# The opening of a two-block transformer layer: the adaptive scale computed on TensorE, products before the norm is known, no GpSimd

## The chip, the cores and the metric

One core of a Trainium2 chip. The metric is the device time of one execution in microseconds (us). All data is fp32; 268 MB of weights are read once from device memory.

## The reference

`reference` runs two blocks on x (256 tokens by 1024 features). Only the start of the first block is touched:

```
ada = silu(c) @ w_ada + b_ada                 # 1024 -> 6 x 1024
sh1, sc1, g1, sh2, sc2, g2 = split(ada, 6)
h = rms_norm(x, norm1_pre) * (1 + sc1) + sh1
proj = h @ w_in                               # ... q, k (512 each), v (1024), c/b/x gates, o, i, f, ga, gm
qk = silu(causal_dwconv(concat(q, k), conv_qk_w))     # 4 taps
```

rms_norm divides each token by the root of its mean square, so it is one factor r per token. The mLSTM over q, k, v, the rest of the mixer, the PEER layer with 16384 experts and the whole second block follow, and the change leaves them as they are.

## The kernel before

Features lie on the 128 partitions, in 8 groups j (or k) of 128; a tile 128x256 is one group of all 256 tokens. Every weight matrix comes from device memory in pieces of 128x1024 fp32 (512 KB). ScalarE rounds a piece to its high part `wh`, VectorE or GpSimd subtracts to get the low part `wl` (`split`, L160), and TensorE makes three products per 128x128 square: `wh`·`hh`, `wh`·`hl`, `wl`·`hh` (`mm3`, L182), where `hh` and `hl` are the two parts of h. 24 such matmuls of 256 columns are one output of 128 features (`gemm`, L189).

The opening is a list of steps, `ORD` (L25), run at L556 in that order; the planner of the language then orders each engine's queue by its own estimate of when an instruction can start.

- `load_c` (C, L461): silu(c) as one row on one partition, ten small matmuls on ones (`F0`), and four matmuls of one row that spread it over all partitions into `crow`.
- `load_x` (X, L500): x, its squares and their sum over features, the factor r per token (L318), and `u` = x·r for the 8 groups on VectorE (L506).
- `load_shift` (B0 to B7, L536) and `load_scale` (S0 to S7, L524): each loads a 128x1024 piece of `w_ada` (rows are features, so the product with silu(c) is a sum along the row) and VectorE multiplies it by `crow` and adds up (`product`, L423). B gives 128 shifts, S gives 128 scales. S then sets gain A1 (L526), ScalarE makes `u`·A1 + B1 (L528) and the high part (L532), GpSimd the low part (L532).
- `load_w` (W0 to W5, L508): pieces of the q and k weights; GpSimd makes five of the six low parts (`WG`, L30). `FL` (L27) adds filler matmuls behind some loads.
- `some` (H, L544): the outputs 0 to 3 group by group as the groups of h come, then 4 and 5.

`ORD2` (L26, run at L650) is what follows: w0, w1 load and split pieces 6 and 7 of the q and k weights; q6, q7 are their outputs; u0 to u7 are the units that take an output out of the accumulator, convolve it over four taps and apply silu (`unit_qk`, L577, with `conv`, L571); v0 to v3 compute v from 8 pieces (`wide`, L195), of which GpSimd makes the low part of every second one (`PV`, L29); l0 and g0 are the gates. Outputs 0, 1, 6, 7 and all of v share two accumulator banks with the name `mm`. After that comes the loop at L717 over the pieces `wcxb`, and from there on the kernel is a long row of such products.

Of the kernel before, what the change touches and what calls it, by code (L numbers as in the profile page):

```python
# [8 lines left out]
F32 = mybir.dt.float32  # L9
F32R = mybir.dt.float32r  # L10
# [102 lines left out]
def body(ctx: ExitStack, tc: tile.TileContext, a: dict):  # L113
# [298 lines left out]
    with ExitStack() as p1:  # L412
# [4 lines left out]
        A.dma_start(out=col, in_=a["cols"])  # L417
        A.dma_start(out=cst["a"], in_=a["ca"])

        def big(name, slot, dt=F32):  # L420
            return f8.tile([128, 8, 256], dt, tag=f"s{slot}", name=name)

        def product(raw, j):  # L423
            scr = m1.tile([128, 1024], F32, tag="adas", name="scr", bufs=2)
# [3 lines left out]
        def adapt():  # L428
            for b in range(16):
                raw = m1.tile([128, 2048], F32, tag="araw", name="araw", bufs=2)  # L430
                SY.dma_start(out=raw, in_=a["wada"][8 + b])
# [12 lines left out]
        u = big("u", 5)  # L444
        qz = big("qz", 2)
        G.memset(qz, 0.0)
# [6 lines left out]
        def bct():  # L453
            return bank("bc", 256)

        banks = [bank(t) for t in ("sc", "num", "den", "ssq", "bc")]
        psb = bank("psb")

        early = []

        def load_c():  # L461

            c1, t1 = (m1.tile([128, 1024], F32, tag="adas", name=n, bufs=2)[:1] for n in ("c1", "t1"))
            tc.keep_in_program_order(SY.dma_start(out=c1, in_=a["c"]))
            A.activation(t1, c1, AF.Tanh, scale=0.5)
            V.scalar_tensor_tensor(out=c1, in0=t1, scalar=1.0, in1=c1, op0=ALU.add, op1=ALU.mult)
            for n in range(F0):
                T.matmul(psb[:, :128], lhsT=ones, rhs=ones, start=True, stop=True)
            for i in range(2):
                early[:] = [T.matmul(banks[i], lhsT=ones[:1, :], rhs=c1[:, i * 512:(i + 1) * 512], start=True, stop=True)]  # L470
                A.copy(crow[:, i * 512:(i + 1) * 512], banks[i])
# [6 lines left out]
        def warm(key, raw):  # L478

            for n in range(FL.get(key, 0)):  # L480
                T.matmul(psb[:, :256], lhsT=ones, rhs=raw[:, n * 256:(n + 1) * 256], start=True, stop=True)

        where = dict(B0=4, B2=8, B4=0, B6=0, S0=6, S2=7, S4=3, S6=0)
        stage = {}

        def adaload(src, t, n):
            b = f"{t}{n & 6}"
            if n % 2 == 0:
                if where[b]:
                    stage[b] = f8.tile([128, 2048], F32, tag=f"s{where[b]}", name="araw")  # L490
                else:
                    stage[b] = m1.tile([128, 2048], F32, tag="araw", name="araw", bufs=2)
            raw = halfload(stage[b], src[n // 2], n % 2)
            warm(f"{t}{n}", raw)
            return raw

        raws = [sp.tile([128, 2048], F32, tag="raw", name="raw", bufs=3) for _ in range(3)]
        ws, more = [], []

        def load_x():  # L500
            tc.keep_in_program_order(SY.dma_start(out=x, in_=a["xT"].rearrange("p (j t) -> p j t", j=8)))
            with tc.issue_after(early[0].ins):
                sums(m1, banks[4], x, presum(m1, x))
                r1 = norm(m1, banks[4])[0]
            for j in range(8):
                V.tensor_mul(u[:, j, :], x[:, j, :], r1)  # L506

        def load_w(n):  # L508
            p = halfload(raws[n // 2], a["wqk"][n // 2], n % 2)
            warm(f"W{n}", p)  # L510
            if n < 4:
                ws.append(split(p, G if WG >> n & 1 else V))
                return
            t = f8.tile([128, 2048], F32R, tag=f"s{(4, 8)[n - 4]}", name="w4")
            with tc.issue_after(made[0].ins), tc.issue_after(made[1].ins):
                A.copy(t[:, :1024], p)
                (G if WG >> n & 1 else V).tensor_sub(t[:, 1024:], p, t[:, :1024].bitcast(F32))
            more.append((t[:, :1024], t[:, 1024:]))

        A1, B1, one = (m1.tile([128, 8], F32, name=n) for n in ("A1", "B1", "one"))  # L520
        V.tensor_scalar_add(one, col[:, bo + 8:bo + 16], 1.0)
        V.tensor_mul(one, one, KS("n1pre"))

        def load_scale(n):  # L524
            product(adaload(a["wada"][4:], "S", n), 8 + n)
            V.scalar_tensor_tensor(out=A1[:, n:n + 1], in0=ada[:, 8 + n:9 + n], scalar=K("n1pre", n), in1=one[:, n:n + 1],  # L526
                                   op0=ALU.mult, op1=ALU.add)
            A.activation(u[:, n, :], u[:, n, :], AF.Identity, scale=A1[:, n:n + 1], bias=B1[:, n:n + 1])  # L528
            parts_of_h(n)

        def parts_of_h(j):
            made[:] = [A.copy(hh[:, j, :256], u[:, j, :]), G.tensor_sub(hl[:, j, :256], u[:, j, :], hh[:, j, :256].bitcast(F32))]  # L532

        made = []

        def load_shift(n):  # L536
            product(adaload(a["wada"], "B", n), n)

        def shift():
            V.tensor_add(B1, ada[:, 0:8], col[:, bo:bo + 8])  # L540

        pss = [mmt(), mmt()] + [b[:, :256] for b in banks[:4]]

        def some():  # L544

            for k in range(8):
                n = slice(k * 128, (k + 1) * 128)
                for i, (x_, w_) in enumerate(((hh, 0), (hh, 1), (hl, 0))):
                    for ps, w in zip(pss, ws):
                        T.matmul(ps, lhsT=w[w_][:, n], rhs=x_[:, k, :256], start=k == 0 and i == 0,  # L550
                                 stop=k == 7 and i == 2)
            for ps, w in zip(pss[4:], more):
                gemm(ps, w, hh, hl)

        raw3 = sp.tile([128, 2048], F32, tag="raw", name="raw", bufs=3)
        for t in ORD.split():  # L556
            {"X": load_x, "C": load_c, "W": load_w, "S": load_scale, "B": load_shift, "F": shift,
             "H": some}[t[0]](*[int(v) for v in t[1:]])
        bg = []
        bg_ada = [adapt()]  # L560

# [87 lines left out]
        cst["b"] = m1.tile([128, NCST["b"]], F32, name="cb")  # L649
        for t in ORD2.split():  # L650
            n = int(t[1])
            if t[0] == "w":
                w67 = split(halfload(raw3, a["wqk"][3], n))
            elif t[0] == "l":
                wif = m1.tile([128, 8, 72], F32, name="wif")
                tc.keep_in_program_order(SY.dma_start(out=wif, in_=a["wif"].rearrange("p (k n) -> p k n", k=8)))
                SY.dma_start(out=cst["b"], in_=a["cb"])
            elif t[0] == "q":
                pss.append(mmt())
                gemm(pss[-1], w67, hh, hl)  # L660
            elif t[0] == "u":
                unit_qk(pss[n], n)
            elif t[0] == "v":
# [769 lines left out]
def layout(x, c, w_ada, b_ada, norm1_pre, norm1_post, w_in, conv_a_w, conv_qk_w, b_igate, b_fgate, mh_norm_w,  # L1433
# [27 lines left out]
    r["wada"] = ca(w.reshape(1024, 24, 2, 128).transpose(1, 3, 2, 0)).reshape(24, 128, 2048)  # L1461
    r["c"] = n(c)
    cols = np.zeros((128, NCOL), np.float32)

    def put(name, v):
# [72 lines left out]
```

## Time and profile before

| | us |
|---|---|
| three runs: median (lowest to highest) | 1509.54 (1508.81 to 1511.1) |
| the profiled execution, its time | 1508.95 |
| span of its instructions | 1507.2 |
| TensorE busy over the span | 1453.8 |
| VectorE busy | 1156.4 |
| ScalarE busy | 906.3 |
| GpSimd busy | 107.2 |

The profile is of one execution. An engine's busy time says how much of the span it worked; the rows further down say when, what ended its waits, and at which clock TensorE ran. PE is TensorE's matmuls, PEld its weight loads, DVE VectorE, ACT ScalarE, POOL GpSimd.

### The profile page before, as it was taken

The numbers are of one execution on the slowest core, as the hardware profiler recorded it, in microseconds if no ns is written. First come the engines' busy times: TensorE is split into PE (matmuls) and PEld (weight loads), VectorE is DVE, ScalarE is ACT, GpSimd is POOL, SyncE is SP. The second block draws the span as 40 slices with busy tenths as digits, with TensorE's granted clock in tenths as the row PEclk, the third lists the DMA queues.
The fourth block names the chain that finished last, engine by engine and source line by source line (L and its number), as shares of the span: only waits on it lengthen the run. The fifth ranks groups of instructions, "written<-read, shape, count | busy, mean of one in ns | idle before, by whom it ended". The sixth has DMA issues, their size and how long they took to land.

```text
span 1507.2 us, 27126 instructions
## 1 busy us (share of the span) xinstructions
PE 1453.8 (96%) x11020; PEld 1324.7 (88%) x11020; DVE 1156.4 (77%) x2154; ACT 906.3 (60%) x1242; POOL 107.2 (7%) x55
## 2 busy tenths in 40 slices
PE   5899999998998799999999999999999999999998
PEld 4889899997998799999878998777788899899897
DVE  8978797667998927787999887888865679575554
ACT  3554354445543547888877777787755569554543
POOL 3310000004231430000000000000000000000000
PEclk8999999999999999999999999999999999999999
DMA  9556667553434364544455545554555643345542
GB/s 349 182 201 231 229 251 255 181 180 119 169 140 168 112 200 166 169 167 169 144 178 182 169 168 172 183 177 168 168 185 183 219 158 128 104 173 199 180 168 84
DMA packets 40015, 268.63 MB, mean 178 GB/s; under 512 B 4561, under 2 KB 5329, under 8 KB 9170
## 3 DMA queue, kind: packets, MB, share of 16 engines
q1 hardware_dynamic: 38882, 264.67, 50.6%
q10 hardware_dynamic: 1008, 2.23, 0.5%
q8 instruction: 86, 1.41, 0.4%
q14 instruction: 39, 0.32, 0.1%
HBM read 265.83 MB, written 1.05 MB: 177 GB/s over the span
## 4 chain that ended last, share of the span: by engine, by line
PE 83%; DVE 13%; ACT 3%; issue 2%; DMA 0%; DVEq 0%; ACTq 0%
PE mm L185 13%; PE mm L187 13%; PE mm L186 13%; PE acc L255 10%; PE acc L256 10%; PE acc L257 10%; PE g L1069 3%; DVE wl L166 2%; DVE pr L936 1%; PE acc L185 1%; PE acc L187 1%; PE acc L186 1%; DVE scr L425 1%; ACT wh L165 1%; PE mm L206 1%
## 5 line engine op out<-in xcount | busy, mean ns | idle before, releaser
L165 ACT CAST wh<-raw 128x1024 fp32r<-128x1024 f32 x450 | 471.2, 1050 | 472.3 <-PE mm L186 223.9
L166 DVE TENSOR_TENSOR wl<-raw,wh 128x1024 fp32r<-128x1024 f32 x415 | 510.4, 1233 | 181.7 <-ACT wh L165 177.3
L185 PE MATMUL mm<-hh,wh 128*128 128x256 f32 x1816 | 520.4, 287 | 4.6 <-ACT z L871 4.6
L187 PE MATMUL mm<-hh,wl 128*128 128x256 f32 x1816 | 514.9, 284 | 10.2 <-DVE wl L166 10.2
L186 PE MATMUL mm<-hl,wh 128*128 128x256 f32 x1816 | 512.5, 282 | 0.0
L187 PEld LDWEIGHTS mm<-hh,wl 128*128 128x128 f32 x1816 | 345.7, 190 | 12.2 <-DVE wl L166 10.8
L185 PEld LDWEIGHTS mm<-hh,wh 128*128 128x128 f32 x1816 | 344.6, 190 | 11.1 <-ACT z L871 5.2
L186 PEld LDWEIGHTS mm<-hl,wh 128*128 128x128 f32 x1816 | 345.1, 190 | 1.3 <-issue 0.2
L255 PE MATMUL acc<-wh,ah 128*128 128x512 f32 x512 | 205.1, 401 | 1.0 <-ACT ah L262 1.0
L256 PE MATMUL acc<-wh,al 128*128 128x512 f32 x512 | 201.8, 394 | 0.0
L257 PE MATMUL acc<-wl,ah 128*128 128x512 f32 x512 | 201.6, 394 | 0.0
L1047 ACT COPY o<-os 128x1024 f16<-128x1024 f16 x96 | 196.9, 2051 | 1.2 <-DVE os L1044 1.2
L166 POOL TENSOR_TENSOR wl<-raw,wh 128x1024 fp32r<-128x1024 f32 x35 | 90.7, 2596 | 435.7 <-PE mm L326 254.4
L257 PEld LDWEIGHTS acc<-wl,ah 128*128 128x128 f32 x512 | 96.2, 188 | 22.3
L255 PEld LDWEIGHTS acc<-wh,ah 128*128 128x128 f32 x512 | 96.1, 188 | 21.7 <-ACT ah L262 1.1
L256 PEld LDWEIGHTS acc<-wh,al 128*128 128x128 f32 x512 | 96.1, 188 | 20.6
L1072 DVE SCALAR_TENSOR_TENSOR z<-g,z 128x256 f32<-128x256 f32 x128 | 51.1, 419 | 45.5 <-PE g L1069 45.3
L1044 DVE TENSOR_TENSOR os<-io,idxT 128x1024 f16<-128x1024 f16 x96 | 66.2, 689 | 21.8 <-ACT o L1047 21.2
L1054 DVE TENSOR_TENSOR og<-o,gT 128x512 f16<-128x512 f16 (+1 forms) x96 | 82.4, 859 | 0.0
L425 DVE SCALAR_TENSOR_TENSOR scr<-araw,crow 128x1024 f32<-128x1024 f32 x48 | 59.7, 1261 | 2.7 <-DMA araw<-in_wada_dram 2.7
L1069 PEld LDWEIGHTS <-o 128*128 128x128 f16 x1536 | 46.4, 96 | 15.5 <-issue 11.9
L1069 PE MATMUL g<-og,o 128*128 128x32 f16 (+1 forms) x1536 | 56.5, 182 | 0.3 <-ACT o L1047 0.3
(444 smaller groups left out, 1962.6 us busy)
## 6 DMA issues: line engine op xcount, KB each, us to landing
raw<-in_uT_dram SPq DMA_DIRECT2D x64, 1024.0 KB, 4.9
raw<-in_ev_dram SPq DMA_DIRECT2D x64, 1024.0 KB, 4.9
araw<-in_wada_dram SPq DMA_DIRECT2D x16, 1024.0 KB, 6.3
raw<-in_wup_dram SPq DMA_DIRECT2D x16, 1024.0 KB, 4.9
raw<-in_wdn_dram SPq DMA_DIRECT2D x16, 1024.0 KB, 4.9
raw<-in_wcxb_dram SPq DMA_DIRECT2D x12, 1024.0 KB, 4.8
araw<-in_wada_dram SPq DMA_DIRECT2D x16, 512.0 KB, 9.9
raw<-in_wout_dram SPq DMA_DIRECT2D x8, 1024.0 KB, 4.9
```

Of the source, the lines that this page charges most:

```text
L165: by.copy(wh, raw) if by is A else by.tensor_copy(wh, raw)
L166: on.tensor_sub(wl, raw, wh)
L185: T.matmul(ps, lhsT=wh, rhs=xh, start=start, stop=False, skip_group_check=skip)
L186: T.matmul(ps[:, :n], lhsT=wh, rhs=xl, start=False, stop=False, skip_group_check=skip)
L187: return T.matmul(ps, lhsT=wl, rhs=xh, start=False, stop=stop, skip_group_check=skip)
L255: T.matmul(acc[t][c], lhsT=xh[:, ts_], rhs=wh[:, cs], start=first and n == 0, stop=False)
L256: T.matmul(acc[t][c], lhsT=xl[:, ts_], rhs=wh[:, cs], start=False, stop=False)
L257: T.matmul(acc[t][c], lhsT=xh[:, ts_], rhs=wl[:, cs], start=False, stop=last and n == len(steps) - 1)
L425: return V.scalar_tensor_tensor(out=scr, in0=raw, scalar=0.5, in1=crow, op0=ALU.mult, op1=ALU.mult, accum_out=ada[:, j:j + 1])
L1047: A.copy(o1, os.rearrange("p n t -> p t n"))
L1054: V.tensor_tensor(out=og, in0=o2[:, :, None, :].to_broadcast([128, TB, 2, m]), in1=gT[:, ts_, :, None].to_broadcast([128, TB, 2, m]), op=A ...
L1069: T.matmul(ps[:, t], lhsT=o1[:, t, :], rhs=og[:, t, i], start=i == 0, stop=i == 1)
```

## The change

The order of the opening becomes S first, with x among it, then B; W6 and W7 join it. x comes in two halves. The shift and the scale are no longer needed before the products: the accumulator of an output takes w·(x·A1) plus, in two more columns (256 and 257), w·B1, and the unit that reads output 0 to 6 multiplies by r and adds the two columns' sum. Scales come from matmuls with the piece of `w_ada` (laid out the other way, `wsc`) as weights and one column of silu(c) as moving data. `scaled` and `biased` (L333, L339) are helpers that the kernel has already: ScalarE makes the high part, VectorE the low part. `plan(at, f)` puts a call behind the step with number `at`.

```diff
-ORD = "C X B0 B1 W0 B2 B3 W1 B4 B5 W2 B6 B7 W3 F S0 S1 S2 S3 S4 S5 S6 S7 W4 W5 H"
-ORD2 = "w0 u0 u1 q6 u2 w1 v0 u6 u3 q7 v1 l0 u4 u7 v2 g0 u5 v3"
-FL = dict(B4=2,B5=2,W2=2,B6=2,B7=2,W3=2,S0=2)
+ORD = "C S0 X0 S1 X1 W0 S2 S3 W1 S4 W2 S5 W3 S6 S7 B0 W4 B1 W5 B2 W6 B3 B4 B5 B6 B7 W7"
+ORD2 = "u0 u1 q7 u2 v0 u3 v1 l0 u4 u7 v2 g0 u5 v3 u6"
-WG = 47
...
+        pss = [pmm.tile([128, 512], F32, tag="mm", name="mm", bufs=2)[:, :258] for _ in range(2)]
+        pss += [bank(t, 258) for t in ("sc", "num", "den", "ssq", "psb")]
+        aux = bank("bc")
...
+        def row_of_c():
+            for i in range(2):
+                for k in range(4):
+                    T.matmul(aux[:, k * 128:(k + 1) * 128], lhsT=cs[:, 4 * i + k:4 * i + k + 1].to_broadcast([128, 128]),
+                             rhs=C("ident"), start=k == 0, stop=k == 3, skip_group_check=True)
+                A.copy(crow[:, i * 512:(i + 1) * 512], aux)
...
+        def sums_of(sq, j):
+            for t in range(2):
+                T.matmul(aux[:, 256 + t:257 + t], lhsT=sq[:, t * 128:(t + 1) * 128], rhs=ones[:, 0:1], start=False,
+                         stop=j == 7, skip_group_check=True)
...
+        def load_w(e, n):
...
+            A.copy(wh, p)
+            ws.append((wh, wl))
+            plan(e + 1, lambda: V.tensor_sub(wl, p, wh.bitcast(F32)))
+            if n < 7:
+                plan(e + 1, first_products, n, None)
+                plan(e + 2, last_products, n, None)
+
+        def load_scale(e, k):
+            raw = adaload(a["wsc"], "S", k)
+            for i in range(8):
+                T.matmul(aux[:, 300 + k:301 + k], lhsT=raw[:, i * 128:(i + 1) * 128], rhs=cs[:, i:i + 1],
+                         start=k == 0 and i == 0, stop=i == 7, skip_group_check=True)
+            plan(e + 1, gain_of, k)
+            plan(max(e + 3, 13), normed_of, k)
+            plan(e + 2, first_products, None, k)
+
+        def gain_of(k):
+            V.scalar_tensor_tensor(out=A1[:, k:k + 1], in0=aux[:, 300 + k:301 + k], scalar=half[:, k:k + 1],
+                                   in1=one[:, k:k + 1], op0=ALU.mult, op1=ALU.add)
+            scaled(x, A1, xh, xl, k)
+
+        def normed_of(k):
+            V.scalar_tensor_tensor(out=u[:, k, :], in0=x[:, k, :], scalar=A1[:, k:k + 1], in1=r1, op0=ALU.mult,
+                                   op1=ALU.mult)
+
+        def load_shift(e, k):
+            product(adaload(a["wada"], "B", k), k)
+            plan(e + 1, shift_of, k)
+            plan(e + 2, last_products, None, k)
+
+        def shift_of(k):
+            V.tensor_add(B1[:, k:k + 1], ada[:, k:k + 1], col[:, bo + k:bo + k + 1])
+            A.copy(xh[:, k, 256:257], B1[:, k:k + 1])
+            V.tensor_sub(xh[:, k, 257:258], B1[:, k:k + 1], xh[:, k, 256:257].bitcast(F32))
+            A.copy(xl[:, k, 256:258], xh[:, k, 256:258])
+            biased(u[:, k, :], B1, hh, hl, k)
...
+        def first_products(n, k):
...
+            for n, k in pairs:
+                T.matmul(pss[n][:, :256], lhsT=ws[n][0][:, k * 128:(k + 1) * 128], rhs=xh[:, k, :256], start=k == 0,
+                         stop=False, skip_group_check=True)
...
+        def last_products(n, k):
...
+            for n, k in pairs:
+                for w_, x_ in ((0, xl), (1, xh)):
+                    T.matmul(pss[n], lhsT=ws[n][w_][:, k * 128:(k + 1) * 128], rhs=x_[:, k, :], start=False,
+                             stop=k == 7 and w_ == 1, skip_group_check=True)
...
         def conv(src, taps, w, out, j):
-            V.tensor_scalar(out=out, in0=src[:, 0:256], scalar1=w(0, j), scalar2=None, op0=ALU.mult)
+            A.activation(out, src[:, 0:256], AF.Copy, scale=w(0, j))
...
         def unit_qk(ps, j):
...
-            A.copy(pad[:, 3:259], ps)
+            if j < 7:
+                V.tensor_reduce(out=B1[:, j:j + 1], in_=ps[:, 256:258], axis=AX.X, op=ALU.add)
+                V.tensor_mul(pad[:, 3:259], ps[:, :256], r1)
+                A.activation(pad[:, 3:259], pad[:, 3:259], AF.Identity, bias=B1[:, j:j + 1])
+            else:
+                A.copy(pad[:, 3:259], ps)
```

The low parts of all W pieces are now VectorE's; W0 to W3 and W7 use the four rotating buffers of `split`, so W7 takes the one that W0 held; W4 to W6 have space of their own. The zeroing of `qz` on GpSimd moves behind the opening. GpSimd keeps the low parts of every second piece of v. The same bytes are loaded.

## Rows read from the trace of the kernel before

**Rows 1.** The page: TensorE over the whole span.
```profile
PE 1453.8 (96%) x11020; PEld 1324.7 (88%) x11020; DVE 1156.4 (77%) x2154; ACT 906.3 (60%) x1242; POOL 107.2 (7%) x55
```
**Rows 2.** Busy time by stretch: length, PE, PEld, DVE, ACT, POOL, granted clock, DMA share, GB/s.
```profile
0.00:34.40 34.40, 18.40 (x60) 13.89 (x60) 27.98 (x45) 12.88 (x21) 12.79 (x9) 0.90 0.91 349
34.40:49.00 14.60, 14.02 (x97) 13.32 (x98) 12.29 (x22) 8.67 (x16) 5.49 (x8) 0.88 0.53 203
49.00:58.20 9.20, 9.20 (x76) 8.87 (x74) 9.14 (x17) 6.79 (x11) 2.49 (x1) 1.00 0.53 171
58.20:80.80 22.60, 15.95 (x120) 15.50 (x119) 21.37 (x37) 9.98 (x22) 7.29 (x3) 0.92 0.59 210
80.80:98.40 17.60, 17.60 (x130) 16.84 (x131) 11.50 (x18) 8.65 (x13) 2.56 (x1) 0.90 0.55 204
98.40:1507.20 1408.80, 1378.59 (x10543) 1256.27 (x10543) 1074.12 (x2021) 859.33 (x1163) 76.56 (x33) 0.99 0.50 173
```
**Rows 3.** Timeline, ScalarE and TensorE: the last copy of v, the first product behind.
```profile
98.42 0.36 ACT L209 COPY v<-mm 128x256 f32<-128x256 f32 x1
98.51 0.28 PE L185 MATMUL mm<-hh,wh 128*128 128x256 f32 x1
```
**Rows 4.** The chain that ended last, two of its pieces in the opening.
```profile
33.29 1.15 DVE scr L425 x2
34.47 0.72 DVE A L526
```
**Rows 5.** Lines L468, L470, L308: count, ns min/median/max, first to last start.
```profile
L468 PE MATMUL psb<-ones x20: 421/421/580, 1.1 to 5.3; 128*128 128x128 f32 x20
L470 PE MATMUL num<-c,ones x2: 1056/1056/1056, 7.5 to 8.4; 1*128 1x512 f32 x2
L308 PEld LDWEIGHTS bc<-ones,total x4: 288/336/338, 11.7 to 12.3; 128*128 128x128 f32 x4
L308 PEld LDWEIGHTS ss<-ones,sq x8: 192/192/192, 354.4 to 355.2; 128*128 128x128 f32 x8
```
**Rows 6.** Busy time of two microseconds, columns as in rows 2.
```profile
37.00:38.00 1.00, 1.00 (x7) 1.00 (x7) 1.00 (x1) 0.93 (x2) 0.00 (x0) 0.53 1.01 414
38.00:39.00 1.00, 1.00 (x10) 1.00 (x10) 0.96 (x4) 0.14 (x2) 0.73 (x1) 1.00 1.05 430
```
**Rows 7.** Timeline, TensorE: start, duration, of every third product of a gemm.
```profile
50.11 0.28 PE L187 MATMUL den<-hh,w 128*128 128x256 f32 x1
...
50.47 0.28 PE L187 MATMUL den<-hh,w 128*128 128x256 f32 x1
```
**Rows 8.** Timeline, ScalarE: two instructions that a load released.
```profile
6.28 0.42 ACT L281 ACTIVATE total<-x 128x256 f32<-128x256 f32 x1 [2.31 <-DMA x<-in_xT_dram]
...
22.00 1.04 ACT L165 CAST wh<-raw 128x1024 fp32r<-128x1024 f32 x1 [2.27 <-DMA raw<-in_wqk_dram]
```
**Rows 9.** Groups by line, VectorE: two of 0 to 49 us, two of 49 to 98.4 us.
```profile
L425 DVE SCALAR_TENSOR_TENSOR scr<-araw,crow 128x1024 f32<-128x1024 f32 x16 | 21.3, 1348 | 0.0
L526 DVE SCALAR_TENSOR_TENSOR A<-ada,col,one 128x1 f32<-128x1 f32 x8 | 5.0, 623 | 0.3
...
L166 DVE TENSOR_TENSOR wl<-raw,wh 128x1024 fp32r<-128x1024 f32 x9 | 11.0, 1218 | 3.2 <-ACT wh L165 3.2
...
L588 DVE SCALAR_TENSOR_TENSOR qz<-cvt,cv 64x256 f32<-64x256 f32 x8 | 3.3, 417 | 0.1
```
**Rows 10.** Lines L572 and L574 to 110 us: count, ns min/median/max, first to last start.
```profile
L572 DVE TENSOR_SCALAR cv<-pad,col x9: 340/347/2497, 49.6 to 107.0; 128x256 f32<-128x256 f32 x9
...
L574 DVE SCALAR_TENSOR_TENSOR cv<-pad,col,cv x26: 467/478/2490, 52.2 to 109.9; 128x256 f32<-128x256 f32 x26
```
**Rows 11.** Timeline, all engines: around the longest wait of TensorE behind the opening.
```profile
58.46 2.35 POOL L166 TENSOR_TENSOR wl<-raw,wh 128x1024 fp32r<-128x1024 f32 x1 [6.61 <-ACT wh L165]
58.62 2.34 DVE L572 TENSOR_SCALAR cv<-pad,col 128x256 f32<-128x256 f32 x1
...
62.15 0.58 PE L206 MATMUL mm<-wl,hh 128*128 128x256 f32 x1 [3.92 <-DVE wl L166]
```

More of the change, by code (lines that the diff above doesn't have):

```diff
@@ L454, in bct @@
             return bank("bc", 256)
[L456 to L471, printed above, removed]
+        pss = [pmm.tile([128, 512], F32, tag="mm", name="mm", bufs=2)[:, :258] for _ in range(2)]
+        pss += [bank(t, 258) for t in ("sc", "num", "den", "ssq", "psb")]
+        aux = bank("bc")
+        xh, xl = (slot_of(n, i, F32R).rearrange("p (j n) -> p j n", j=8) for n, i in (("xh", 6), ("xl", 7)))
+        u = big("u", 5)
+        A1, B1, one, half, cs, ct = (m1.tile([128, 8], F32, name=n) for n in ("A1", "B1", "one", "half", "cs", "ct"))
+        rc = m1.tile([128, 4], F32, tag="rc", name="rc", bufs=1)
+        r1 = m1.tile([128, 256], F32, name="r1")
+        raws = [sp.tile([128, 2048], F32, tag="raw", name="raw", bufs=3) for _ in range(3)]
+        raws.append(None)
+        stage, ws, done, low = {}, [], [], []
         def halfload(raw, src, i):
@@ L476, in halfload @@
             return raw[:, h_]
[L478 to L484, printed above, removed]
         def adaload(src, t, n):
-            b = f"{t}{n & 6}"
+            b = (t, n // 2)
             if n % 2 == 0:
-                if where[b]:
-                    stage[b] = f8.tile([128, 2048], F32, tag=f"s{where[b]}", name="araw")
+                if b in (("S", 0), ("S", 3), ("B", 2)):
+                    stage[b] = slot_of("araw", 8)[:, :2048]
@@ L491, in adaload @@
                 else:
                     stage[b] = m1.tile([128, 2048], F32, tag="araw", name="araw", bufs=2)
[L493 to L506, printed above, removed]
@@ L508, in load_w @@
-        def load_w(n):
-            p = halfload(raws[n // 2], a["wqk"][n // 2], n % 2)
[L510 to L558, printed above, removed]
+            return halfload(stage[b], src[n // 2], n % 2)
+        agenda = {}
+        def plan(at, f, *args):
+            agenda.setdefault(at, []).append((f, args))
+        def load_c(e, _):
+            A.activation(ct, KS("c"), AF.Tanh, scale=0.5)
+            V.scalar_tensor_tensor(out=cs, in0=ct, scalar=1.0, in1=KS("c"), op0=ALU.add, op1=ALU.mult)
+            V.tensor_scalar_add(one, col[:, bo + 8:bo + 16], 1.0)
+            V.tensor_mul(one, one, KS("n1pre"))
+            V.tensor_scalar_mul(half, KS("n1pre"), 0.5)
+            for n in range(F0):
+                T.matmul(pss[6][:, :128], lhsT=ones, rhs=ones, start=True, stop=True)
+            plan(e, row_of_c)
@@ new lines, in row_of_c, with load_x @@
+        def row_of_c():
[4 more added lines that the diff above has]
+                A.copy(crow[:, i * 512:(i + 1) * 512], aux)
+        def load_x(e, n):
+            js = slice(4 * n, 4 * n + 4)
+            tc.keep_in_program_order(SY.dma_start(out=x[:, js, :], in_=a["xT"].rearrange("p (j t) -> p j t", j=8)[:, js, :]))
+            for i in range(2):
+                plan(e + 3 + i, squares_of, e + 3 + i, 4 * n + 2 * i)
+            if n:
+                plan(e + 7, norm_of)
@@ new lines, in squares_of, with norm_of @@
+        def squares_of(e, j0):
+            for j in range(j0, j0 + 2):
+                sq = m1.tile([128, 256], F32, tag="sq", name="sq", bufs=4)
+                A.activation(sq, x[:, j, :], AF.Square)
+                plan(e + 1, sums_of, sq, j)
+        def sums_of(sq, j):
+            for t in range(2):
+                T.matmul(aux[:, 256 + t:257 + t], lhsT=sq[:, t * 128:(t + 1) * 128], rhs=ones[:, 0:1], start=False,
+                         stop=j == 7, skip_group_check=True)
+        def norm_of():
+            A.activation(rc[:, 0:2], aux[:, 256:258], AF.Sqrt, bias=epsc, scale=1.0 / D)
+            V.reciprocal(rc[:, 2:4], rc[:, 0:2])
+            for t in range(2):
+                T.matmul(aux[:, t * 128:(t + 1) * 128], lhsT=rc[:, 2 + t:3 + t].to_broadcast([128, 128]), rhs=C("ident"),
+                         start=False, stop=t == 1, skip_group_check=True)
+            A.copy(r1, aux[:, :256])
@@ new lines, in load_w @@
+        def load_w(e, n):
+            if n == 6:
+                raws[3] = sp.tile([128, 2048], F32, tag="raw", name="raw", bufs=3)
+            p = halfload(raws[n // 2], a["wqk"][n // 2], n % 2)
+            if n < 4 or n == 7:
+                sps.append(sps.pop(0))
+                nb = sps.count(sps[0])
+                wh, wl = (sps[0].tile([128, 1024], F32R, tag=t, name=t, bufs=nb) for t in ("wh", "wl"))
+            else:
+                t = f8.tile([128, 2064], F32R, tag=f"s{n - 2}", name="w4")
+                wh, wl = t[:, :1024], t[:, 1024:2048]
+            A.copy(wh, p)
[4 more added lines that the diff above has]
+                plan(e + 2, last_products, n, None)
@@ new lines, in body @@
+        ready_w, ready_s, ready_b = [], [], []
+        def first_products(n, k):
+            if n is None:
+                ready_s.append(k)
+                pairs = [(i, k) for i in ready_w]
+            else:
+                ready_w.append(n)
+                pairs = [(n, i) for i in ready_s]
+            for n, k in pairs:
+                T.matmul(pss[n][:, :256], lhsT=ws[n][0][:, k * 128:(k + 1) * 128], rhs=xh[:, k, :256], start=k == 0,
+                         stop=False, skip_group_check=True)
@@ new lines, in last_products @@
+        def last_products(n, k):
+            if n is None:
+                ready_b.append(k)
+                pairs = [(i, k) for i in low]
+            else:
+                low.append(n)
+                pairs = [(n, i) for i in ready_b]
+            for n, k in pairs:
+                for w_, x_ in ((0, xl), (1, xh)):
+                    T.matmul(pss[n], lhsT=ws[n][w_][:, k * 128:(k + 1) * 128], rhs=x_[:, k, :], start=False,
+                             stop=k == 7 and w_ == 1, skip_group_check=True)
@@ L559, in body @@
+        for e, t in enumerate(ORD.split()):
+            {"X": load_x, "C": load_c, "W": load_w, "S": load_scale, "B": load_shift}[t[0]](e, int(t[1:] or 0))
+            for f, args in agenda.pop(e, ()):
+                f(*args)
+        for e in sorted(agenda):
+            for f, args in agenda[e]:
+                f(*args)
+        qz = big("qz", 2)
+        G.memset(qz, 0.0)
         bg = []
@@ L651, in body @@
             n = int(t[1])
-            if t[0] == "w":
-                w67 = split(halfload(raw3, a["wqk"][3], n))
-            elif t[0] == "l":
+            if t[0] == "l":
                 wif = m1.tile([128, 8, 72], F32, name="wif")
@@ L1460, in layout @@
     w = n(w_ada)[0]
-    r["wada"] = ca(w.reshape(1024, 24, 2, 128).transpose(1, 3, 2, 0)).reshape(24, 128, 2048)
-    r["c"] = n(c)
+    wa = np.concatenate([w[:, :1024], w[:, 2048:]], 1)
+    r["wada"] = ca(wa.reshape(1024, 20, 2, 128).transpose(1, 3, 2, 0)).reshape(20, 128, 2048)
+    r["wsc"] = colchunks(w, [1024 + 128 * i for i in range(8)])
     cols = np.zeros((128, NCOL), np.float32)
```

12 lines of the change are left out of this document (6 added, 6 removed).

## Prediction

> **What bounds the kernel now.** I read the page first: TensorE is busy for 96% of the span [rows 1]. The stretches say where the rest lies [rows 2]: behind 98.4 us it works 1378.6 of 1408.8 us, and it is there, at 98.4, that v is done and the loop over `wcxb` begins [rows 3]. So what counts is when TensorE gets to that point; a microsecond there is a microsecond of the span, because all that follows is TensorE's own work with its loads ahead of it.
>
> Ahead of 98.4 the reader is to see three parts. To 34.4 us TensorE has no product of the gemms to make. To 49.0 it is paced by VectorE: the chain goes through pairs of a scale product and a gain, 1.15 and 0.72 us [rows 4], eight times. To 58.2 it runs without a gap (outputs 4, 5 and 6, 72 products, then three of v's): the seven outputs stand at about 57.8. From there to 98.4 are 40.6 us, in which TensorE has output 7, v and the gates to make, 24 + 192 + 24 = 240 products. One product of 256 columns costs 0.12 us at the full clock (0.36 us for three [rows 7]), so that is 28.8 us of work; 11.8 us are waits and a low clock. VectorE is the one waited for: it works 21.4 of the 22.6 us from 58.2 to 80.8 [rows 2], and part of that is standing still beside GpSimd. The first tap of the convolution takes 0.35 us alone and 2.35 while GpSimd subtracts [rows 10, 11].
>
> **The opening after the change, on TensorE.** All loads come in the same 512 KB pieces: 12 of them between x and W3, from 6.28 to 22.0 us, 1.31 us each [rows 8]. S0 and X0 take the place of x, so S7 lands at about 22, B7 at 22 + 11 x 1.31 = 36.4, W7 at 37.7. TensorE's own work is longer, so it sets the end:
> - The ten filler matmuls stay, to 5.7 us [rows 5]. The row of silu(c) is 8 matmuls, 16 passes of 0.22 us (the spacing of the filler: 4.2 us over 19 gaps [rows 5]), with two copies of some 0.6 us between; from about 6.7, when x landed before, it ends at 11.4 (estimates from these rows).
> - Eight scale pieces: 64 matmuls of one column, two passes each, 128 passes. The nearest thing in the trace is the sum of squares, L308, also a 128x128 weight load and one column: 0.114 us per pass at 354 us (0.8 us over 7 gaps), 0.2 at 11.7 us (0.6 over 3) [rows 5]. That is 14.6 us at the 2.4 GHz level or 25.6 at the 1.2 level.
> - Squares: 32 such passes, 3.6 or 6.4 us; norm 0.5.
> - 56 first products and 112 last ones at 0.12 us: 20.2.
> - Scales, sums, norm and row of c all lie in one accumulator bank, `aux`. VectorE's eight gains and ScalarE's reads of it stand between TensorE's writes: ten hand-overs that the trace of before does not show. From below 0.2 us each (2 us), from above the rest of a 1.2 us VectorE instruction in front plus the read, 1.4 (14 us; 1.2 is L166's mean [rows 9]). VectorE is not full there, so I take 0.4 each, 4 us.
>
> At the high level the sum is 11.4 + 14.6 + 3.6 + 0.5 + 20.2 + 4 = 54.3 us for the seven outputs, against 57.8: 3.5 us earlier.
>
> VectorE hides below that. It loses 8 of 16 products (1.35 us each with the GpSimd waits, 21.3 in all), the eight products x·r and the waits in the gains (0.62 where such a small operation needs about 0.2) [rows 9]. It gains seven low parts at 1.22, and three passes of about 0.45 us over each group. That is some 34 us of work spread over 5 to 54. ScalarE gets the small copies; its share in these stretches was 21.6 of 49 us [rows 2], so it covers them. If that cover went, last products would wait for the low parts of h.
>
> For the clock, the trace first: from 1.1 to 9.4 us TensorE had instructions without a gap, the filler and then matmuls of a single row, and all of them ran at the 1.2 GHz level: the last of them still took 1.06 us for 512 columns [rows 5]. Ordinary products, on the other hand, brought it to 2.4 within 3.5 us: seven in one microsecond at 37, ten in the next, granted clock 0.53 and 1.00 [rows 6]. What matmuls of one column do for it no row shows. The Trainium skill, page "TensorE: Matmul & The Clock Gate", Part 1, says that the low clock is the default and that recent activity of TensorE lifts it; by that rule the scale matmuls, which leave no idle time, keep it high and the sum is 54.3, by the first rows it is some 16 us more (the first rival).
>
> **Behind the opening.** (a) W7 takes W0's buffer, which is free only with W0's last product: rounding 1.04 [rows 8], subtraction 1.22 [rows 9], hand-overs of about 0.3, in which TensorE has nothing to do: 2.6 us lost. What queues behind is q7 and v on TensorE. In the old order the splits of pieces 6 and 7 ran under outputs 4 and 5. (b) The wait of 3.9 us at 58.2, for a low part of v that stood behind a tap blocked by GpSimd [rows 11], goes: the first piece of v is split while q7's 24 products (2.9 us) run. Late next is the second piece, GpSimd's, 2.35 us, inside the same cover. (c) The units get longer on VectorE: seven times a reduction of two columns (0.15, as the smallest operations) and a product out of the accumulator (0.42, as L588 [rows 9]), +4.0; eight first taps of 0.35 go to ScalarE, -2.8. The tap that GpSimd blocked is gone, the wait isn't: the taps behind it, L574, also reach 2.49 us against a median of 0.48 [rows 10], and GpSimd keeps four pieces of v. I charge the 1.2 us difference in part, 0.8. (d) Outputs 7 and v share two banks, and u7 now comes late; that delays v by a copy per tile, but the old order had the same waits; zero, up to 3 us if it doesn't. (e) Taps on ScalarE in the later loop over `wcxb`: covered by TensorE's products; zero.
>
> Sum: 3.5 - 2.6 + 3.9 - 0.8 = 4.0 us earlier at 98.4. The profiled execution took 1508.95 (span 1507.2 and 1.75 around it), so 1504.95; its time stands 0.6 under the median of the three runs, so I forecast **1505.5**. Its own range, with 0.2 to 0.8 us per hand-over, is 1500 to 1509.
>
> **Rivals.**
> - *The clock stays low through the scales* (slower). 160 passes of one column cost 0.086 us more each, 13.8, and the first products of W0 to W3 among them (32 at 0.09) 2.9: 16.7 us. The lead of 4.0 turns into 12.7 behind, 1521 to 1522 for the median; as the splits of v and part of the waits behind the opening then have more time, 1514 to 1521, say 1517. For it: TensorE at 1.2 GHz through 8 us of gapless work at the start [rows 5]. Against: ordinary products stand between the scales. It decides from about 45 passes at the low level on (4.0 / 0.086) and is measurable from 80.
> - *VectorE ends the stage* (about no change). From 49.0 to 98.4 it worked 42.0 us [rows 2]. Without the splits of W4 and W6 (1.8), one wait beside GpSimd (2.0, W5's) and with (c), +1.2, it has 39.4 left, but begins with none of the units done at 54.3 where it began at 49.0: 93.7 against 91.0, 2.7 later. If the units go ahead of v's low parts, this eats the lead: 1508 to 1512, say 1510. For it: VectorE's 95% from 58.2 to 80.8. Against: v's low parts can slip in while a unit waits for ScalarE.
> - *The waits behind the opening go* (a larger gain). If only 4 of the 11.8 us of waits are left, TensorE is through at 54.3 + 2.6 + 28.8 + 4 = 89.7, 8.7 us earlier, and with quick hand-overs 10 to 11: 1499. For it: no split of q and k but one is left there. Against: the same VectorE work.
>
> The bank's upper bound (14 us, +10) would look like the first rival. The Trainium skill, page "PSUM — Partial Sum Buffer", "PSUM bank collisions raise a hardware error", has two engines kept apart by bank even on other columns, which speaks against the one shared bank; no row here prices it.
>
> **Numbers.** A measurement of this kernel can tell about 0.2%, 3 us, from no change. Forecast 0.42 (0.36 of it faster by more than that), clock 0.28, VectorE 0.20 (0.16 within), larger gain 0.10. So faster 0.46, same 0.22, slower 0.32. The range goes from the larger gain to above the middle of the clock's case: 1497 to 1519.
>
> **What would show it.** Right: W7's split behind the last product of output 0, v's first product within 7 us of the seventh output, passes of the scales 0.11 us apart, the first product of `wcxb` near 94. Wrong: passes 0.2 apart and a granted clock of 0.5 between 12 and 40 us; VectorE's gains with long idle times released by TensorE; TensorE waiting for VectorE behind the opening for over 10 us; GpSimd still beside a blocked VectorE in the opening; a gap of the loads before 36 us that TensorE then waits for.

## The result: slower, and the profile after

The changed kernel takes 1534.87 us (median of 4 runs, 1533.25 to 1535.88) against 1509.17 for the kernel before, beside which it ran: a ratio of 1.0169 (95% interval 1.0153 to 1.0185), 25.7 us more. The forecast was 1505.5 with a range up to 1519; the first rival happened, and cost more than it was priced at.

The page's head and the busy time by stretch (columns as in [rows 2]):

```profile
span 1531.4 us, 27425 instructions
PE 1481.2 (97%) x11160; PEld 1354.4 (88%) x11160; DVE 1142.1 (75%) x2166; ACT 915.5 (60%) x1274; POOL 88.5 (6%) x42
```
```profile
5.00:10.00 5.00, 2.11 (x13) 1.66 (x12) 0.45 (x4) 1.53 (x5) 0.00 (x0) 0.98 1.02 409
10.00:58.00 48.00, 42.90 (x194) 41.70 (x194) 11.30 (x23) 11.46 (x21) 0.00 (x0) 0.50 0.49 176
58.00:78.00 20.00, 17.43 (x120) 16.84 (x120) 18.80 (x49) 9.97 (x29) 0.00 (x0) 0.84 0.82 308
```

A higher busy share of TensorE, 97 against 96%, goes with a slower kernel: its instructions last longer. From 10 to 58 us the granted clock is 0.50, the 1.2 GHz level, while TensorE works 42.9 of 48 us. VectorE has 11.3 us of work in those 48 us, and works 18.8 of the next 20. The loads move 176 GB/s where they moved 349 at the start of the kernel before [rows 2]: their queue waited four times, 43.3 us in all, until the scale passes had read the pieces in the buffers.

The timeline of the changed kernel, TensorE (start, duration, count of passes, idle time before it), and VectorE's last gains:

```profile
1.08 4.64 PE L496 MATMUL psb<-ones 128*128 128x128 f32 x20 [1.08 <-DVE pad L637]
7.93 1.13 PE L502 MATMUL bc<-ca,cs 128*128 128x128 f32 x8 [2.21 <-DMA ca<-in_ca_dram]
9.74 2.08 PE L502 MATMUL bc<-ca,cs 128*128 128x128 f32 x8 [0.68 <-ACT crow L504]
12.49 3.58 PE L554 MATMUL bc<-cs,araw 128*128 128x1 f32 x16 [0.68 <-ACT crow L504]
16.45 3.57 PE L554 MATMUL bc<-cs,araw 128*128 128x1 f32 x16 [0.39 <-DVE A L561]
...
40.05 1.70 PE L522 MATMUL bc<-ones,sq 128*128 128x1 f32 x8
...
55.28 3.41 PE L554 MATMUL bc<-cs,araw 128*128 128x1 f32 x16
...
81.35 0.28 PE L605 MATMUL psb<-xh,w 128*128 128x258 f32 x1
```
```profile
58.72 0.22 DVE L561 SCALAR_TENSOR_TENSOR A<-bc,half,one 128x1 f32<-128x1 f32 x1 [5.17 <-PE bc L554]
...
60.40 0.21 DVE L561 SCALAR_TENSOR_TENSOR A<-bc,half,one 128x1 f32<-128x1 f32 x1
```

Sixteen scale passes take 3.4 to 3.6 us, 0.21 to 0.22 each, from the first piece to the last. The clock was low before they began. Of passes with 128 columns, 20 of the filler take 4.64 us, the first eight of the row of c 1.13 and the next eight 2.08: low, high, and low again from about 9.8 us, 2.7 us ahead of the first scale pass.

```profile
9.00:10.00 1.00, 0.33 (x2) 0.26 (x2) 0.00 (x0) 0.90 (x3) 0.00 (x0) 0.89 1.05 422
10.00:11.00 1.00, 1.00 (x6) 1.00 (x7) 0.00 (x0) 0.61 (x3) 0.00 (x0) 0.50 1.00 336
```

So the scale passes did not bring the level down in this kernel; it stayed low under them. Ahead of the first change in this trace the granted clock reads 1.00 in the filler too, so there the durations decide. A mean over a whole run can mislead in the same way: one of the four runs lists 0.989, the others 0.971 to 0.973, and it is the slowest.

The last gain of VectorE stands at 60.4 us, and the last product of the seven outputs at 81.35, where 54.3 was forecast and the kernel before had 57.8. The last copy of v starts at 122.83 us, 24.4 later than in [rows 3], and the span is 24.2 us longer. So nearly the whole loss, 23.6 us, stands ahead of the last product of the seven outputs.

Behind the opening, TensorE's waits from 81 us on (line, releaser: us in total, times, longest), and the two instructions behind the longest wait for VectorE:

```profile
PE mm L203 <- ACT v L208: 4.5, 2, 3.4
PE mm L205 <- DVE wl L165: 2.7, 1, 2.7
PE mm L186 <- DVE wl L546: 0.6, 1, 0.6
```
```profile
84.73 2.40 POOL L165 TENSOR_TENSOR wl<-raw,wh 128x1024 fp32r<-128x1024 f32 x1 [1.65 <-ACT wh L164]
```
```profile
85.20 3.02 DVE L165 TENSOR_TENSOR wl<-raw,wh 128x1024 fp32r<-128x1024 f32 x1
```

### The profile page after: what moved, and what is told of

The parts are those of the page before. It is cut to its first block, busy times and chain, and to the rows that moved or that the text cites. A ratio compares the mean times of both kernels' runs of the same rounds, so it can differ in the third digit from the quotient of the medians.

```text
span 1531.4 us, 27425 instructions
## 1 busy us (share of the span) xinstructions
PE 1481.2 (97%) x11160; PEld 1354.4 (88%) x11160; DVE 1142.1 (75%) x2166; ACT 915.5 (60%) x1274; POOL 88.5 (6%) x42
## 4 chain that ended last, share of the span: by engine, by line
PE 82%; DVE 12%; ACT 3%; issue 1%; DMA 0%; DVEq 0%; ACTq 0%
PE mm L184 13%; PE mm L186 12%; PE mm L185 12%; PE acc L254 10%; PE acc L255 10%; PE acc L256 10%; PE g L1130 3%; DVE wl L165 2%; PE bc L554 1%; DVE pr L997 1%; PE acc L184 1%; PE acc L186 1%; PE acc L185 1%; DVE cv L632 1%; ACT wh L164 1%
## 5 line engine op out<-in xcount | busy, mean ns | idle before, releaser
L164 ACT CAST wh<-raw 128x1024 fp32r<-128x1024 f32 x444 | 465.1, 1049 | 466.0 <-PE mm L185 206.3
L186 PEld LDWEIGHTS mm<-hh,wl 128*128 128x128 f32 x1808 | 344.3, 190 | 11.7 <-DVE wl L165 9.5
L165 POOL TENSOR_TENSOR wl<-raw,wh 128x1024 fp32r<-128x1024 f32 x31 | 79.9, 2579 | 415.5 <-PE mm L325 252.1
L262 DVE TENSOR_TENSOR al<-z,ah 128x256 fp32r<-128x256 f32 x128 | 53.2, 418 | 1.8 <-ACT ah L261 1.8
```

Source lines behind the costliest of these rows:

```text
L164: by.copy(wh, raw) if by is A else by.tensor_copy(wh, raw)
L165: on.tensor_sub(wl, raw, wh)
L186: return T.matmul(ps, lhsT=wl, rhs=xh, start=False, stop=stop, skip_group_check=skip)
```

## Experiments

All times are medians beside the kernel before on the same chip (1509.5, 1509.3, 1509.1 and 1508.9 us in the four groups). The theory was that the passes of one column let TensorE's clock fall and keep it low. The rivals were the shared bank, too little work per pass at any clock, and VectorE.

**The bank alone.** The scale results go to the accumulator bank of the seventh output, everything else stays (`...` marks what is left out of a line). In this kernel and in the next two the sum of squares is added onto what the row of c left in its bank, so the norm factor is another number; no instruction is added or left out by that.

```diff
-                T.matmul(aux[:, 300 + k:301 + k], ..., rhs=cs[:, i:i + 1],
+                T.matmul(sbank[:, 64 * k:64 * k + 1], ..., rhs=cs[:, i:i + 1],
```


> The results of the scale matmuls go to a bank of their own (the one that output 6 takes later); all else as in the changed kernel. Clock theory (the one-column passes leave TensorE at 1.2 GHz, and that is most of the 25 us): granted clock still 0.5 from 10 to 60 us, passes still 0.22 us apart, time within 4 us of the changed kernel's 1535. Hand-over theory (the shared bank makes TensorE wait for VectorE and ScalarE): 8 waits of 0.4 to 1 us go, and squares no longer stand between scales: 5 to 10 us faster, 1525 to 1530.

One run: 1531.61 us, 3.3 less than the median of the changed kernel and 1.6 less than its fastest run. The granted clock is the same 0.50:

```profile
10.00:15.00 5.00, 5.00 (x25) 5.00 (x25) 0.70 (x2) 2.01 (x5) 0.00 (x0) 0.50 1.02 402
35.00:40.00 5.00, 4.01 (x17) 3.63 (x18) 1.70 (x5) 1.44 (x2) 0.00 (x0) 0.50 0.76 283
```

By this one run the hand-overs through one bank cost some 3 us; most of the loss is not there.

**64 columns in the scale passes.** The same bank, each scale matmul moves 64 equal columns.

```diff
+                T.matmul(sbank[:, 64 * k:64 * k + 64], ...,
+                         rhs=cs[:, i:i + 1].to_broadcast([128, 64]),
```


> As e1_bank, but each scale matmul moves 64 equal columns in place of one; weight loads, passes and order of data stay, and 64 columns still take less than the weight load at the low clock. Clock theory, with the number of moving columns as what TensorE's clock looks at: granted clock 1.00 within the scales, passes 0.11 to 0.13 us apart, the seven outputs 15 to 20 us earlier, 1512 to 1520. If columns don't matter, or the hand-overs or VectorE are the cause: as e1_bank within 2 us.

1529.39 us (ratio 1.0142, 1.0107 to 1.0176); the four runs lie in two pairs, 1524.6 and 1524.9, 1533.8 and 1534.3. The time stands near the second expectation, but the trace shows both levels. The profiled run is one of the lower pair. TensorE's timeline there, and three single microseconds of it:

```profile
11.89 2.00 PE L555 MATMUL psb<-cs,araw 128*128 128x64 f32 x16 [0.31 <-DVE A L563]
13.72 4.26 PE L523 MATMUL bc<-ones,sq 128*128 128x1 f32 x32
17.85 0.78 PE L594 MATMUL mm<-xh,wh 128*128 128x256 f32 x2
18.42 3.51 PE L555 MATMUL psb<-cs,araw 128*128 128x64 f32 x16
```
```profile
15.00:16.00 1.00, 1.00 (x11) 1.00 (x10) 0.49 (x1) 1.00 (x4) 0.00 (x0) 1.00 1.02 418
16.00:17.00 1.00, 1.00 (x10) 1.00 (x9) 0.00 (x0) 1.00 (x2) 0.00 (x0) 0.82 1.03 422
17.00:18.00 1.00, 1.00 (x6) 1.00 (x7) 0.90 (x1) 0.98 (x2) 0.00 (x0) 0.50 1.04 426
```

The first pieces run at the high level, 16 passes in 2.0 us. Then come the 32 one-column passes of the square sums, a gapless 4.3 us, and the clock falls among them, near 16.6 us: eleven passes start in the microsecond from 15, six in the one from 17. So passes of one column have no fixed price of 0.22 us; the level sets it. Behind them the same 16 passes take 3.51, and the granted clock stays at 0.50 from 20 to 35 us.

**The scale on VectorE again.** The rest of the change stays (order, early products, no GpSimd in the opening). The piece lies in memory as the shifts' pieces do, and the gain reads VectorE's sum.

```diff
-            raw = adaload(a["wsc"], "S", k)
-            for i in range(8):
-                T.matmul(aux[:, 300 + k:301 + k], lhsT=raw[...], rhs=cs[:, i:i + 1], ...)
+            product(adaload(a["wsc"], "S", k), 8 + k)
```


> The scale is made by VectorE again, by the product with the row of silu(c); first products, norm put in at the unit, and all the rest as in the changed kernel. Clock theory: 128 passes of 0.22 us (28 us) leave TensorE, VectorE takes 8 products of 1.2 us in a stretch where it stood idle for over half of the time: 1505 to 1515. VectorE theory (VectorE sets the end of the opening and of the stage behind): 10 us more for VectorE, 1540 or more.

1512.78 us (ratio 1.002, 1.0011 to 1.003). Its stretch from 20 to 55 us:

```profile
20.00:55.00 35.00, 24.70 (x138) 22.41 (x139) 34.56 (x79) 15.71 (x39) 0.00 (x0) 0.72 0.85 305
```

VectorE is full, 34.6 of 35 us, and the loss against before is 3 us, as the clock theory had it: the one-column passes on TensorE cost 22 us more than the work that they took off VectorE.

**128 columns throughout.** Scale passes and square sums move 128 columns: the same matmuls, the same products, the scales in the bank of the first experiment. The square sums get columns of their own, so the norm is whole again.

```diff
-                T.matmul(aux[:, 300 + k:301 + k], ..., rhs=cs[:, i:i + 1],
+                T.matmul(sbank[:, 128 * (k % 4):128 * (k % 4) + 128], ...,
+                         rhs=cs[:, i:i + 1].to_broadcast([128, 128]),
...
-                T.matmul(aux[:, 256 + t:257 + t], ..., rhs=ones[:, 0:1],
+                T.matmul(aux[:, 256 + 128 * t:384 + 128 * t], ..., rhs=ones[:, 0:128],
```


> The changed kernel with every matmul between the row of c and the first product moving 128 columns instead of one: the 64 scale matmuls (128 passes) move 128 equal columns of cs into the bank of the seventh output, and the 16 matmuls of the square sums (32 passes) move 128 columns of ones. No instruction more, no product more. Theory (the clock: the one-column passes let it fall to 1.2 GHz at 10 us and kept it there): granted clock near 1.00 from 5 us on, 16 scale passes in 1.8 to 2.0 us instead of 3.5, scales done near 42 instead of 58 us, first products at the high level; time 1534 less 14 to 20 us, 1510 to 1520, and near 1505 if the sum of the prediction holds apart from its clock. Rival (the level falls whatever the passes move, as it fell behind 32 one-column square passes with 64-column scales beside them): granted clock 0.50 from 12 to 50 us, 16 passes in 3.5 us or more, 1529 to 1536.

1507.78 us (ratio 0.999, 0.998 to 0.9999): 27.1 us less than the changed kernel. Its stretches, then TensorE's timeline and the line of the gains (count, ns min/median/max, first to last start):

```profile
10.00:32.00 22.00, 22.00 (x191) 21.84 (x191) 11.86 (x24) 12.51 (x23) 0.00 (x0) 1.00 0.99 375
32.00:50.00 18.00, 15.13 (x115) 13.90 (x114) 17.18 (x47) 8.06 (x27) 0.00 (x0) 1.00 0.87 326
```
```profile
7.67 2.05 PE L503 MATMUL bc<-ca,cs 128*128 128x128 f32 x8 [1.95 <-DMA ca<-in_ca_dram]
...
10.95 1.05 PE L503 MATMUL bc<-ca,cs 128*128 128x128 f32 x8
...
15.10 1.06 PE L523 MATMUL bc<-ones,sq 128*128 128x128 f32 x8
...
16.34 1.95 PE L556 MATMUL psb<-cs,araw 128*128 128x128 f32 x16
...
54.12 0.28 PE L607 MATMUL psb<-xh,w 128*128 128x258 f32 x1
```
```profile
L563 DVE SCALAR_TENSOR_TENSOR A<-psb,half,one x8: 206/218/220, 12.9 to 32.8; 128x1 f32<-128x1 f32 x8
```

The granted clock is 1.00 from 10 to 50 us, a pass with 128 columns takes some half of the time of a pass with one, and the last gain comes at 32.8 us, 27.6 earlier. (The first half of the row of c, at 7.67 us, still ran at the low level.) The last product of the seven outputs comes at 54.1, where the prediction had 54.3. The run with the bank alone differs from this kernel in the moved columns and in where the square sums lie, and the time differs by 23.8 us: the clock was the cause of most of the loss, some 3 us go with the bank. The expectation has the one-column passes let the clock fall at 10 us. By the rows of the result it fell ahead of the scale passes there; what they did was to leave it low, where passes of 128 columns ran high.

**64 columns, square sums of 128.** As the last kernel, but 64 columns in the scale passes.

```diff
-                         rhs=cs[:, i:i + 1].to_broadcast([128, 128]),
+                         rhs=cs[:, i:i + 1].to_broadcast([128, 64]),
```


> As the kernel with 128 columns throughout, but the scale matmuls move 64; the square sums still move 128. It tells what brought the clock down in the earlier run with 64-column scales, whose square sums moved one column: the clock fell there at 18 us, in the 4.3 us of 32 one-column passes. If those were the cause: granted clock near 1.00 from 5 to 60 us and a time like the kernel with 128 columns, 1505 to 1520. If 64 columns are too few by themselves: granted clock 0.50 again from 20 us at the latest until the products begin, 1524 to 1534.

1517.84 us (ratio 1.0055, 1.0038 to 1.0071). The time lies in the first expectation's range, its runs reach from 1511.3 to 1520.8, and the granted clock went as neither has it: 0.50 from 10 to 19 us, 1.00 from 20 to 50. TensorE's timeline:

```profile
13.83 3.67 PE L556 MATMUL psb<-cs,araw 128*128 128x64 f32 x16 [0.31 <-DVE A L563]
17.30 4.15 PE L523 MATMUL bc<-ones,sq 128*128 128x128 f32 x26
...
21.73 1.89 PE L556 MATMUL psb<-cs,araw 128*128 128x64 f32 x16
```

Here the clock fell near 9.2 us, half a microsecond into the first 64-column passes, rose under the 26 passes of square sums with 128 columns, and the later 64-column passes ran at the high level. In the earlier kernel the same passes ran high first and low behind the one-column sums. So passes of 64 columns were seen at both levels, and with them the time scatters by 10 us. What decides between the levels there stays open.

**The first tap on ScalarE, alone.** The kernel before with that part of the change only.

```diff
-            V.tensor_scalar(out=out, in0=src[:, 0:256], scalar1=w(0, j), ...)
+            A.activation(out, src[:, 0:256], AF.Copy, scale=w(0, j))
```


> The kernel before with one part of the change alone: the first tap of the convolutions on ScalarE. If the wait beside GpSimd merely moves to the next VectorE instruction: 0.35 us less for VectorE in each of 8 units, one hop more to ScalarE: within 3 us of 1509. If the tap in its fast mode was the one that stood still: 5 waits of 2 us go, 4 to 8 us faster.

1507.65 us (ratio 0.9984, 0.9974 to 0.9993): within 3 us, as the first expectation has it.

**No GpSimd in the opening, alone; and both.** The kernel before with the low parts of its opening on VectorE, without and with the tap.

```diff
-WG = 47
+WG = 0
-    made[:] = [A.copy(...), G.tensor_sub(hl[:, j, :256], ...)]
+    made[:] = [A.copy(...), V.tensor_sub(hl[:, j, :256], ...)]
```


> The kernel before with no GpSimd in the opening alone; the first tap stays on VectorE. With the tap on ScalarE as well it gave 1504.4, and the tap alone 1507.65 against 1509.5. If the two parts add: 1506 to 1507. If the freed VectorE time of the tap is what makes room for the low parts: 1508 to 1512.

> The kernel before with two parts of the change alone: no GpSimd in the opening (all low parts of weights and of the input computed by VectorE) and the first convolution tap on ScalarE. The tap alone gave 1507.65 (ratio 0.9984). If GpSimd's instructions hold VectorE up in the opening (shared port), as the taps of 2.4 to 3.3 us beside them suggest: 1500 to 1506. If VectorE becomes the end of the opening instead (eight low parts of the input and five of the weights more on it, some 13 x 0.4 to 1.1 us): 1508 to 1518, with VectorE full from 40 to 65 us.

1504.75 us alone (ratio 0.9974, 0.9965 to 0.9984) and 1504.40 with the tap (0.9965, 0.9955 to 0.9975). The first is faster than both of its expectations, the second is in the range of its first. (Of the 2.4 to 3.3 us in the second expectation, single taps took up to 2.66; the 3.35 was a product in the opening.) Taking GpSimd out is worth 4 us although VectorE gets its work; the tap adds nothing clear of noise to that.

**No GpSimd subtraction behind the opening either.** The low parts of v, in the kernel with 128 columns and in the one just shown, the kernel before with the tap and no GpSimd in its opening.

```diff
-PV = (1,3,5,7)
+PV = ()
```


> The kernel with 128 columns throughout, and no GpSimd behind the opening either: the low parts of the four v weights that GpSimd makes (2.4 to 3.2 us each, during which one VectorE instruction lasts 2.6 to 3.0 us instead of 0.5 to 1.2) are made by VectorE (1.22 us each). If GpSimd holds VectorE up there: VectorE gives 4 x 1.22 and gets back 4 x about 2, a gain of 2 to 4 us, 1503.5 to 1506. If VectorE is simply full and the four are added: a loss of up to 5 us, 1508 to 1513.

> The kernel before with no GpSimd in the opening and the first tap on ScalarE (1504.4), and the four low parts of the v weights on VectorE as well. If GpSimd holds VectorE up there: 1501 to 1503.5. If the added work counts: 1505 to 1509.

1502.07 us (ratio 0.9954, 0.9937 to 0.997) and **1496.42** (0.9911, 0.9895 to 0.9928), both faster than expected. With GpSimd (the kernel with 128 columns), on both engines:

```profile
57.51 2.38 POOL L165 TENSOR_TENSOR wl<-raw,wh 128x1024 fp32r<-128x1024 f32 x1 [1.71 <-ACT wh L164]
...
57.97 3.00 DVE L165 TENSOR_TENSOR wl<-raw,wh 128x1024 fp32r<-128x1024 f32 x1
```

Without it (the same kernel, v on VectorE), group of the line from 53 to 98 us:

```profile
L165 DVE TENSOR_TENSOR wl<-raw,wh 128x1024 fp32r<-128x1024 f32 x13 | 15.8, 1218 | 0.1
```

The same subtraction lasts 3.00 us on VectorE while GpSimd subtracts, and 1.22 without. Four of them go from GpSimd to VectorE, and the last copy of v still comes 9.4 us earlier, at 88.0 (the profiled spans differ by 8.2 us, the medians by 5.7). In the second of the two kernels TensorE has hardly a wait left between 50 and 85 us, and the last copy of v starts at 85.3:

```profile
50.00:85.00 35.00, 34.57 (x284) 33.51 (x282) 29.73 (x59) 23.93 (x44) 0.00 (x0) 1.00 0.69 250
L209 ACT COPY v<-mm x8: 363/368/373, 59.1 to 85.3; 128x256 f32<-128x256 f32 x8
```

The Trainium skill, page "GPSIMD Engine Reference", "1. Specifications", has GpSimd's interfaces to the on-chip memory shared with VectorE, with contention for VectorE instructions that take two inputs there. These rows agree, 3.00 against 1.22 us for a subtraction of two such tiles. The second kernel beats both the one before and the changed one, and none of it is the scale on TensorE.

**The units as before.** With 128 columns, with GpSimd and without, each unit gets back its one copy, so that norm and shift are missing from seven outputs.

```diff
-            if j < 7:
+            if j < 0:
```


> The kernel with 128 columns throughout, with the units that read the seven outputs as they were before: one ScalarE copy into the padded row in place of the reduction, the product with the norm and the biased copy. Norm and shift are therefore missing from seven of the eight outputs; all else stays. It prices the new part of the units (0.15 + 0.41 us of VectorE each, 14 instructions, 3.9 us) in the stage behind the seven outputs, which takes 43.9 us there against 40.6 in the kernel before. If that part is what the stage pays: the last copy of v at 93.5 to 95 us instead of 97.4, time 1504 to 1506. If the stage waits for the low parts of the v weights and the low clock instead, or the first tap (on ScalarE) is late: 1507 to 1509.

> The kernel with 128 columns throughout and the low parts of v on VectorE (1502.07, last copy of v at 88.4 us), with the units as they were before, one ScalarE copy each: norm and shift are missing from seven of the eight outputs. With GpSimd subtracting beside it, leaving the new part of the units out gave nothing (1509.5 against 1507.8). If VectorE's work sets the end of the stage once GpSimd is gone: the 3.9 us of the new part come back in full or in part, last copy of v at 84.5 to 87, time 1498 to 1500.5. If the stage then waits for something else (TensorE's own 28.8 us of products and the hand-over of the last weight): 1501.5 to 1503.

1509.49 us (ratio 1.0001, 0.9991 to 1.0011) with GpSimd, which is no gain on 1507.78: VectorE's next subtraction stands 3.43 us beside GpSimd in place of 3.00.

```profile
57.47 3.43 DVE L165 TENSOR_TENSOR wl<-raw,wh 128x1024 fp32r<-128x1024 f32 x1
```

Without GpSimd 1500.16 (0.9943, 0.9927 to 0.996) against 1502.07, with intervals that overlap, and the last copy of v came at 89.2, not earlier: the time is in the first expectation's range, the copy is not. The new part of the units costs between nothing and 2 us; which of the two is not settled.

## Why the prediction was wrong

**The step that failed** is "At the high level the sum is 11.4 + 14.6 + 3.6 + 0.5 + 20.2 + 4 = 54.3 us". Its two terms for passes of one column, 14.6 and 3.6, were taken at 2.4 GHz, from a row at 354 us where eight such passes stand among other work. In the opening they ran at 1.2 GHz: 27.9 us for the scales and 7.3 for the squares. The rows that spoke against it, TensorE gapless at the low level for 8 us and four such passes 0.2 us apart at 11.7 [rows 5], were in hand and became a rival with a chance of 0.28. The rule of the Trainium skill that the prediction weighed (page "TensorE: Matmul & The Clock Gate", Part 1) did not hold here: TensorE worked 42.9 us of 48, mostly on passes of one column, and the clock stayed at 0.50 for 46 us of them; in the kernel with 64 columns it fell under them. The measurement decides.

**The rival's price** was too low as well: 16.7 us, where the last gain came 27.6 us later than with 128 columns. By the rows of both kernels: eight scale pieces at 3.58 against 1.95 us, 13; four groups of eight square sums at 1.70 against 1.06, 2.6; 24 first products ahead of the last piece at some 0.1 more, 2.4; the norm's four passes at 1.23 against 0.61, 0.6; and 5.1 us in which TensorE stood idle from 10 to 58 us, against none up to 32. That is some 24 of the 27.6. The row of c took the same in both, one half high and one low. The rival then let the late stage absorb part of it. It could not: from the last gain to the last product it is 21.0 us in the changed kernel and 21.3 with 128 columns, because VectorE's eight shift products, each before one group of last products, stand behind the gains in its queue: the first starts at 58.9 us, between the last two gains, though the loads of its piece and the next were issued at 31.0 and 31.8 us and no load of these pieces took more than 10.1 to land. VectorE stood idle for 36.7 us, waiting in order for gains that TensorE was late with, and had its work left when they came. So a late scale moved the whole opening.

**Other steps.**
- Passes 0.2 us at the low level: 0.22. Row of c at 11.4: its second half ran to 11.8. Right.
- Hand-overs on the shared bank, 4 us between 2 and 14: the bank is worth some 3 us in one run. Right in size.
- Loads with B7 at 36.4 us: wrong, since the pieces hold their buffers; in the changed kernel the last load of a shift piece was issued at 63.9 us, and its product ran at 74.7.
- "VectorE hides below that": not quite, even at the high clock. From 32 to 50 us it is nearly full (17.2 of 18) and TensorE stands for 2.9 us. The 54.1 us came out because the hand-overs, charged 4 us, cost almost nothing ahead of that with the scale in another bank (TensorE works 22.00 of 22 us), so two errors cancelled, and that the 54.3 was met is luck.
- (a) W7's split, 2.6: 0.6 measured. W0's last product is not the last of all, and the rounding ran under those of the other outputs.
- (b) "The wait of 3.9 us at 58.2 goes": it came back as 2.7 us for the same kind of low part, again beside GpSimd, at 85.2. The step named GpSimd's subtraction as covered; it is VectorE's beside it that is late. This holds with 128 columns too (2.7 there), and the stage behind the seven outputs took 43.3 us against 40.1 forecast.
- (c) 0.8 for the units: between 0 and 2. (e) zero for the tap: 1.9 us gained by itself, nothing once GpSimd is out.
- (d) zero for the late u7, up to 3: TensorE's waits for the copies of v grew from 2.0 to 4.5 us, 2.5 more.
- *VectorE ends the stage* was half right: with 128 columns the time is 1507.8, just under that rival's 1508 to 1512 and above the main case's 1505.5.

## What to carry to other kernels

Price moved work on TensorE at both clock levels, and take the level from a row where the engine did the same kind of pass for as long; a busy engine is not enough. Look at what stands behind a late input in an engine's queue: here VectorE's shift products stood behind the late gains, and its 36.7 idle us ahead of them did not help. Where GpSimd works beside VectorE on large subtractions, try it without GpSimd first: here that alone was worth more than the whole restructuring.

## What was not expected of the hardware

- A pass of 128 columns took less time than a pass of one: 16 in 1.95 against 3.58 us, since the granted clock was 1.00 with the one and 0.50 with the other. Moving 127 copies of a column that nobody reads made the kernel 27 us faster (with the bank in it, which is some 3).
- The clock fell from 1.00 to 0.50 during 4.3 us of gapless one-column passes (the square sums at 13.7 us in the kernel with 64 columns), and 46 us of mostly such passes did not raise it in the changed kernel.
- With 64 columns the same instructions ran at either level (16 passes in 2.00 and in 3.67 us) in two kernels that are alike up to there, and run times scattered by 10 us.
- Removing four GpSimd subtractions of 2.4 to 3.2 us, and giving them to VectorE, freed 8 us in the best kernel (1504.40 to 1496.42).
